# Fixed slots for the modulation weights, and zero-padded rotary keys, in a one-layer decoder kernel

## The chip, the core and the metric

The kernel runs on one core of a Trainium2 chip. The core has a matrix engine (TensorE, PE in the tables; its weight loads are listed apart as PEld), a vector engine (DVE), an activation engine (ACT), a general engine (GpSimd, POOL) and a queue engine that here only issues transfers (SP). All of them work from on-chip memory with 128 partitions (rows); the matrix engine writes to eight accumulator banks of 128 x 512 float32, which DVE and ACT read. The metric is the device time of one execution in microseconds (us); smaller is better. It is given as the median of several executions. The profile shows one execution.

## What is computed

One decoder layer on 512 tokens with 2048 channels, batch 1, all in float32:

```
mod = silu(c) @ W_ada + b_ada             # 6 vectors of 2048: shift, scale, gate, twice
h   = RMSNorm(x) * (1 + scale_a) + shift_a
proj = h @ W_in                           # q/k/v of mixer A, its indexer, latents of mixer B, two gates
o_A = sparse attention: 8 heads, 2 kv heads, the 128 best keys per query by an indexer
o_B = latent attention: 8 heads, query and key = 128 plain + 64 rotated dimensions
y   = (sigmoid(g_a) * (o_A @ W_pA) + sigmoid(g_b) * (o_B @ W_pB)) @ W_o
x   = x + gate_a * y
h   = RMSNorm(x) * (1 + scale_f) + shift_f
x   = x + gate_f * (W_down( silu(conv(h W_up)_gate) * conv(h W_up)_value ))
```

The change touches two places of this: the logits of mixer B, which for each head are the sum of a product over 128 plain dimensions and one over 64 rotated dimensions,

```
logits[q, s] = sum_{d<128} qn[q, d] kn[s, d] + sum_{r<64} qr[q, r] kr[s, r]
```

and the way in which parts of `W_ada` (2048 x 12288) reach the vector engine.

## The kernel before

Large products are made of three matrix-engine passes, since each float32 operand is split into a rounded part (`hi`) and a rest (`lo`), and hi*hi, hi*lo and lo*hi are summed (`mm3`, lines 141 to 144). A weight tile of 128 x 1024 is loaded by SP into one of five raw buffers, split by ACT (line 130) and DVE (line 131) into one of three hi/lo buffers, and then used (`wtile`, lines 117 to 135). Attention itself (logits, transposes, product with the values) uses plain float32 matmuls, each of which the trace shows as two records.

The rest of the on-chip memory is 81 slots of 128 x 512 float32. `get()` (lines 69 to 76) takes, among the free slots, the one that has rested longest by a counter that stands still during the stages told here, so that free slots are in fact taken first in, first out; `put()` (lines 81 to 86) gives one back. The program text only fixes which slot each tile has and what depends on what. The order of the instructions on each engine is made when the program is built, by a planner that simulates the engines: it takes whatever is ready, by priority, and priority is the order in the text, except that weight tiles are moved 4000 places ahead. After that each engine and each queue runs its list strictly in order and waits where an operand isn't there.

The stages, in order of time in the profile: the projections (to about 430 us), mixer A with the gate projections (to about 780), mixer B's attention together with the product `W_pA` (about 785 to 1060), the product `W_pB` (to about 1130), the product `W_o` (to about 1307), then the feed-forward part (to the end). These parts are touched or spoken of:

- **Modulation stream.** Two thirds of `W_ada` aren't needed at once. `ada_stream` (lines 726 to 755) is a generator that goes through 16 blocks of 512 columns; each of its steps loads two tiles of 128 x 512 (256 KB each; one pair) and has DVE multiply each by its element of silu(c) and add it to an accumulator (lines 745 and 747, three accumulators in turn). `ticker(rate)` calls it `rate` times per weight step of the product running. A pair goes either into two slots (line 735, when `ada_in_slots` is set) or into one of the five raw weight buffers (line 739). The slots are those that `get()` gives next, so the stream walks through the whole free list. Slots are used in mixer A and, from line 1245 on, for the products `W_pB` and `W_o`; the raw buffers in between.
- **Flush.** When a block's accumulator is finished, `flush_cols` (lines 777 to 794) splits it, sums it over the partitions with two matmuls (lines 782 and 783) into the bank that is passed in (the fourth of the next half of the banks) and takes the result out with DVE (lines 790, 793 and 298). The product that follows uses the same bank.
- **Rotated parts of mixer B.** `up_pair(hp)` (lines 1135 to 1208) makes queries and keys of two heads. The rotated parts of both heads stand side by side, 64 columns each, in one tile, and are transposed together, so that `kTr` and `qTr` hold the first head in rows 0 to 63 and the second in rows 64 to 127 (`kTr` at lines 1161 and 1167 to 1170). In `attend_pair` (lines 1210 to 1225), each logit block is a matmul over 64 rows of these tiles (line 1217) and one over the 128 rows of the plain part (line 1218), into the same bank.
- **Attention of a head** (`attend_p`, `attend_pv`, lines 677 to 714): four logit blocks, with 512, 384, 256 and 128 keys; scaled, masked and searched for the extreme by DVE (line 689), exponentiated by ACT (690), normalised by DVE (691, 692), transposed (700), copied out (703, 705), multiplied with the values (708), copied out and split (710, 711).
- **Loads by POOL.** POOL issues stores and reloads of intermediate tiles (lines 713, 714, 804, 805, 822, 1263 to 1265, 1304) and computes small powers (`rsqrt_mean`, line 246), all in one queue.

Of the kernel before, what the change touches and what calls it, by code (L numbers as in the profile page):

```python
# [14 lines left out]
AF = mybir.ActivationFunctionType  # L15
# [16 lines left out]
def trunk_layer_kernel(  # L32
# [48 lines left out]
    def put(*ts, lag=2):  # L81

        for t in ts:
            i = held.pop(id(t))
            rested[i] = clock[0] + lag
            free.append(i)
# [440 lines left out]
    b = bank[7]  # L527
# [194 lines left out]
    ada_acc = [get(), get(), get()]  # L722

    ada_in_slots = [False]

    def ada_stream():
        for n, cb in enumerate(ada_blocks):
            assert len(pend) < 3
            acc = ada_acc[n % 3]
            for kp in range(8):  # L730
                if ada_in_slots[0]:
                    ts = [get(), get()]
                    for i in range(2):
                        k = kp * 2 + i
                        SP.dma_start(ts[i], w_ada[k * P:(k + 1) * P, cb * 512:(cb + 1) * 512])
                else:
                    raw = rawq.popleft()
                    t = raw[:, 0:1024].rearrange("p (k n) -> p k n", k=2)
                    SP.dma_start(t, w_ada[kp * 2 * P:(kp + 1) * 2 * P, cb * 512:(cb + 1) * 512]
                                 .rearrange("(k p) n -> p k n", p=P))  # L740
                    ts = [t[:, 0], t[:, 1]]
                for i in range(2):
                    k = kp * 2 + i
                    if k == 0:
                        V.tensor_scalar(acc, ts[i], c_act[:, 0:1], None, op0=ALU.mult)
                    else:
                        V.scalar_tensor_tensor(acc, ts[i], c_act[:, k:k + 1], acc,  # L747
                                               op0=ALU.mult, op1=ALU.add)
                if ada_in_slots[0]:
                    put(*ts)  # L750
                else:
                    rawq.append(raw)
                yield None
            pend.append((cb, acc))
            done[0] += 1
# [379 lines left out]
    def up_pair(hp):  # L1135
# [22 lines left out]

        lin_tm(w_mkv_up, hp * 512, 512, kvT, 2, MM, ev_up)
        kT = [get(), get()]  # L1160
        kTr = get()
        for a in range(2):
            b = at_bank()
            for tb in range(4):
# [2 lines left out]
        b = at_bank()  # L1167
        for tb in range(4):
            PE.transpose(b[:, tb * P:(tb + 1) * P], kr[:, tb * P:(tb + 1) * P], ident)
        A.activation(kTr, b, AF.Copy)  # L1170
        put(*kn)
        put(kr)

# [36 lines left out]
    def attend_pair(hp):  # L1210
        qT, qTr, kT, kTr, vv, nsc_b, two = pairs.pop(hp)
        for a in range(2):
            rs = slice(a * 64, (a + 1) * 64)

            def qk(o, qb, S, a=a, rs=rs, qT=qT, qTr=qTr, kT=kT, kTr=kTr):
                qs = slice(qb * P, (qb + 1) * P)
                PE.matmul(o[:, :S], qTr[rs, qs], kTr[rs, :S], start=True, stop=False)
                PE.matmul(o[:, :S], qT[a][:, qs], kT[a][:, :S], start=False, stop=True)  # L1218

            attend(qk, lambda qb: Z[:, 384 - qb * P:512], lambda qb, a=a, n=nsc_b: n[:, qb, a:a + 1],  # L1220
                   lambda kc, a=a, vv=vv, two=two: two(vv, kc)[:, a, :], *(ob_d[hp * 2 + a] if hp < 3 else (None, None)))
        put(*vv)
        put(*kT)
        put(*qT)
        put(kTr, qTr)


    pa_d = [dram.tile([P, T], F32, name=f"pa{k}") for k in range(KD)]
# [13 lines left out]
        if hp < 2:  # L1242
            up_pair(hp + 2)
    attend_free("pt")
    ada_in_slots[0] = True
    for t in oa:
        put(*t)
    for t in kvT + mqT:
# [80 lines left out]
        lin_tm(w_o, db * 512, 512, mg, KD, bk, ev_o(db), tick=ticker(TO))  # L1329
    while next(stream, 0) is None:  # L1330
        pass
    for db in range(3):
        x1_T(db, half() if db % 2 == 0 else bk)
        if db == 0:
            for t in mg:
                put(*t)
# [289 lines left out]
```

## Time and profile before

| | |
|---|---|
| median of 3 executions | 2678.14 us (2677.77 to 2680.52) |
| the profiled execution | 2681.41 us |
| its span, first to last instruction | 2679.6 us |
| PE busy | 2604.5 us (97%), 17168 matmul records |
| DVE busy | 2175.6 us (81%) |
| ACT busy | 1265.8 us (47%) |
| POOL busy | 364.2 us (14%) |
| moved by the DMA engines | 464.31 MB, mean 173 GB/s |
| mean granted clock of the matrix engine | 0.99 |

Busy shares are sums over the span. A matmul record begins when the matmul is issued and its end is modelled, so records overlap, and time in which the matrix engine waits inside a record counts as busy. Where an engine waits, the rows name what ended the wait ("<-"); "issue" is a wait for nothing that the profile shows. In rows of groups, the numbers after the bar are the busy time in us, the mean of one instruction in ns and the idle time before them in us.

### The profile page before, as it was taken

The page shows a single profiled execution, that of the slowest core. Times are in us where ns is not written, and L with a number is a line of the kernel's source. Part 1 is how long each engine was busy: PE and PEld are TensorE (multiplying, and loading weights), DVE is VectorE, ACT ScalarE, POOL GpSimd, SP SyncE. Part 2 cuts the span into 40 slices and gives each one's busy share as a digit, 9 for nine tenths or more (in the row PEclk, how much of TensorE's full clock was granted, in tenths as well). Part 3 has the DMA queues.
Part 4 walks back from the last instruction along what each step waited for, and adds up shares of the span by engine and source line. Part 5 has one row for each costly group of instructions (what it writes and reads, how often), then busy time and mean ns, then how long its engine had stood idle before and what let it go on. Part 6 is the DMA issues. An engine that isn't in the chain of part 4 may idle for free.

```text
span 2679.6 us, 44954 instructions
## 1 busy us (share of the span) xinstructions
PE 2604.5 (97%) x17168; PEld 2344.1 (87%) x17168; DVE 2175.6 (81%) x3491; ACT 1265.8 (47%) x1967; POOL 364.2 (14%) x663
## 2 busy tenths in 40 slices
PE   6999999999999999999999999999999999999999
PEld 5777687778997766788789999999999998999999
DVE  7976976779878676984569989989989889878787
ACT  4333434334435556322445555555555556655454
POOL 1000011010022223100100000000001024413120
PEclk8999899999999999999999999999999999999999
DMA  9953136674675587982424343344344447867563
GB/s 341 342 160 104 32 107 204 201 223 155 198 248 171 168 264 246 315 289 93 142 79 136 119 143 124 119 146 126 121 139 148 132 147 212 214 159 205 142 204 116
DMA packets 215661, 464.31 MB, mean 173 GB/s; under 512 B 23786, under 2 KB 65156, under 8 KB 215444
## 3 DMA queue, kind: packets, MB, share of 16 engines
q1 hardware_dynamic: 170260, 344.93, 40.3%
q0 software_dynamic: 45152, 116.50, 15.0%
q8 instruction: 134, 2.20, 0.3%
q14 instruction: 83, 0.68, 0.1%
q10 hardware_dynamic: 32, 0.01, 0.0%
HBM read 397.11 MB, written 64.23 MB: 172 GB/s over the span
## 4 chain that ended last, share of the span: by engine, by line
PE 71%; issue 12%; DMA 8%; DVE 6%; POOL 2%; ACT 2%; SPq 0%; POOLq 0%; DVEq 0%; ACTq 0%
PE bank L1072 13%; PE bank L1074 13%; PE bank L1073 13%; PE bank L142 9%; PE bank L143 9%; PE bank L144 9%; DMA slot<-in_w_ada 3%; DMA x<-slot 2%; DVE whl L139 1%; DMA raw<-in_w_ada 1%; DVE slot L747 1%; DVE slot L572 0%; PE bank L708 0%; DVE raw L968 0%; PE bank L1218 0%
## 5 line engine op out<-in xcount | busy, mean ns | idle before, releaser
L1072 PE MATMUL bank<-slot,whl 128*128 128x256 f32 x3920 | 1104.7, 283 | 24.2 <-ACT slot L972 6.4
L1073 PE MATMUL bank<-slot,whl 128*128 128x256 f32 x3920 | 1101.0, 282 | 0.2 <-DVE slot L139 0.2
L1074 PE MATMUL bank<-slot,whl 128*128 128x256 f32 x3920 | 1090.4, 282 | 7.0 <-DVE whl L139 7.0
L138 ACT ACTIVATE whl<-raw 128x1024 fp32r<-128x1024 f32 (+2 forms) x560 | 532.6, 953 | 620.3 <-PE bank L1073 402.2
L1072 PEld LDWEIGHTS bank<-slot,whl 128*128 128x128 f32 x3920 | 740.4, 189 | 31.4 <-ACT slot L972 9.0
L1073 PEld LDWEIGHTS bank<-slot,whl 128*128 128x128 f32 x3920 | 741.8, 189 | 0.6 <-DVE slot L139 0.5
L1074 PEld LDWEIGHTS bank<-slot,whl 128*128 128x128 f32 x3920 | 734.1, 189 | 8.3 <-DVE whl L139 8.2
L139 DVE TENSOR_TENSOR whl<-raw,whl 128x1024 fp32r<-128x1024 f32 (+2 forms) x560 | 606.0, 1088 | 123.5 <-ACT whl L138 120.8
L130 ACT ACTIVATE whl<-raw 128x1024 fp32r<-128x1024 f32 (+4 forms) x182 | 187.4, 1031 | 381.6 <-PE bank L144 190.5
L968 DVE TENSOR_TENSOR raw<-raw 128x1024 f32<-128x1024 f32 (+2 forms) x320 | 347.5, 1086 | 7.8 <-DMA raw<-in_w_ups 4.9
L131 DVE TENSOR_TENSOR whl<-raw,whl 128x1024 fp32r<-128x1024 f32 (+4 forms) x182 | 216.0, 1188 | 155.2 <-ACT whl L130 149.7
L143 PE MATMUL bank<-whl,slot 128*128 128x512 f32 (+2 forms) x768 | 297.3, 388 | 0.9 <-DVE whl L131 0.9
L142 PE MATMUL bank<-whl,slot 128*128 128x512 f32 (+2 forms) x768 | 292.2, 392 | 4.2 <-ACT slot L409 3.6
L144 PE MATMUL bank<-whl,slot 128*128 128x512 f32 (+2 forms) x768 | 293.0, 386 | 0.0
L142 PE MATMUL bank<-slot,whl 128*128 128x512 f32 (+1 forms) x656 | 264.3, 407 | 7.1 <-DVE slot L790 4.8
L143 PE MATMUL bank<-slot,whl 128*128 128x512 f32 (+1 forms) x656 | 264.0, 403 | 1.8 <-DVE slot L711 1.8
L144 PE MATMUL bank<-slot,whl 128*128 128x512 f32 (+1 forms) x656 | 259.1, 402 | 0.0
L747 DVE SCALAR_TENSOR_TENSOR slot<-slot,c_act,slot 128x512 f32<-128x512 f32 x203 | 148.6, 747 | 37.2 <-DMA slot<-in_w_ada 35.6
L142 PEld LDWEIGHTS bank<-whl,slot 128*128 128x128 f32 x768 | 146.3, 191 | 35.4 <-ACT slot L409 3.7
L143 PEld LDWEIGHTS bank<-whl,slot 128*128 128x128 f32 x768 | 146.4, 191 | 29.8 <-DVE whl L131 1.4
L144 PEld LDWEIGHTS bank<-whl,slot 128*128 128x128 f32 x768 | 144.8, 189 | 29.3 <-issue 0.4
L142 PEld LDWEIGHTS bank<-slot,whl 128*128 128x128 f32 (+1 forms) x656 | 123.5, 188 | 38.1 <-DVE slot L790 5.7
(288 smaller groups left out, 2730.3 us busy)
## 6 DMA issues: line engine op xcount, KB each, us to landing
slot<-in_w_ada SPq DMA_DIRECT2D x344, 256.0 KB, 5.6
raw<-in_w_ups SPq DMA_DIRECT2D x160, 512.0 KB, 5.1
raw<-in_w_in SPq DMA_DIRECT2D x50, 512.0 KB, 3.7
raw<-in_w_down SPq DMA_DIRECT2D x64, 384.0 KB, 3.8
raw<-in_w_down SPq DMA_DIRECT2D x64, 320.0 KB, 3.8
slot<-f POOLq DMA_DIRECT2D x154, 128.0 KB, 4.0
f<-slot POOLq DMA_DIRECT2D x66, 256.0 KB, 5.1
raw<-in_w_gs SPq DMA_DIRECT2D x32, 512.0 KB, 4.6
```

What stands on the lines that cost most here:

```text
L130: A.activation(hi, raw[:, :w], AF.Copy)
L131: V.tensor_tensor(lo, raw[:, :w], r32(hi), ALU.subtract)
L138: A.activation(dst_hi, src, AF.Copy)
L139: V.tensor_tensor(dst_lo, src, r32(dst_hi), ALU.subtract)
L142: PE.matmul(o, lh, rh, start=first, stop=False)
L143: PE.matmul(o, lh, rl, start=False, stop=False)
L144: PE.matmul(o, ll, rh, start=False, stop=last)
L747: V.scalar_tensor_tensor(acc, ts[i], c_act[:, k:k + 1], acc, op0=ALU.mult, op1=ALU.add)
L968: V.tensor_tensor(o[:, :W], a[:, :W], b[:, :W], op)
L1072: PE.matmul(o, wh[:, ks], rh, start=first and k == 0, stop=False, skip_group_check=True)
L1073: PE.matmul(o, wh[:, ks], rl, start=False, stop=False, skip_group_check=True)
L1074: PE.matmul(o, wl[:, ks], rh, start=False, stop=last, skip_group_check=True)
```

## The change

Two edits. First, when the second run of slots begins (line 1245), the modulation stream takes six slots and keeps them: a pair takes the two that stand first in a queue of six and puts them back at its end, so that a pair always follows the pair three before it in the same two slots. The six go back to the free list when the stream has ended, after the product `W_o`. Second, `kTr` becomes two tiles, one per head, each 128 rows high: GpSimd fills the rows of the other head with zeros, ACT copies the head's own 64 rows in, and the matmul over the rotated part runs over all 128 rows, with the queries of both heads in `qTr` as before.

```diff
     ada_in_slots = [False]
+    ada_ring_on, ada_ring = [False], deque()
...
                 if ada_in_slots[0]:
-                    ts = [get(), get()]
+                    ts = [ada_ring.popleft(), ada_ring.popleft()] if ada_ring else [get(), get()]
                     for i in range(2):
                         k = kp * 2 + i
                         SP.dma_start(ts[i], w_ada[k * P:(k + 1) * P, cb * 512:(cb + 1) * 512])
...
-                if ada_in_slots[0]:
+                if ada_ring_on[0]:
+                    ada_ring.extend(ts)
+                elif ada_in_slots[0]:
                     put(*ts)
...
         kT = [get(), get()]
-        kTr = get()
+
+        kTr = [get(), get()]
+        for a in range(2):
+            G.memset(kTr[a][(1 - a) * 64:(2 - a) * 64], 0.0)
...
-        A.activation(kTr, b, AF.Copy)
+        for a in range(2):
+            A.activation(kTr[a][a * 64:(a + 1) * 64], b[a * 64:(a + 1) * 64], AF.Copy)
...
         for a in range(2):
-            rs = slice(a * 64, (a + 1) * 64)
-
-            def qk(o, qb, S, a=a, rs=rs, qT=qT, qTr=qTr, kT=kT, kTr=kTr):
+
+            def qk(o, qb, S, a=a, qT=qT, qTr=qTr, kT=kT, kTr=kTr):
                 qs = slice(qb * P, (qb + 1) * P)
-                PE.matmul(o[:, :S], qTr[rs, qs], kTr[rs, :S], start=True, stop=False)
+                PE.matmul(o[:, :S], qTr[:, qs], kTr[a][:, :S], start=True, stop=False)
                 PE.matmul(o[:, :S], qT[a][:, qs], kT[a][:, :S], start=False, stop=True)
...
-        put(kTr, qTr)
+        put(*kTr, qTr)
...
     attend_free("pt")
-    ada_in_slots[0] = True
+
+    ada_in_slots[0] = ada_ring_on[0] = True
+    ada_ring.extend(get() for _ in range(6))
     for t in oa:
         put(*t)
...
     while next(stream, 0) is None:
         pass
+    put(*ada_ring)
     for db in range(3):
```

## The prediction

> **What bounds the kernel now.** I read the page first, then the span cut at the stages that the change touches, then who waited for whom on each engine there, and last the chain of waits.
>
> ```profile
> span 2679.6 us, 44954 instructions
> PE 2604.5 (97%) x17168; PEld 2344.1 (87%) x17168; DVE 2175.6 (81%) x3491; ACT 1265.8 (47%) x1967; POOL 364.2 (14%) x663
> PE 71%; issue 12%; DMA 8%; DVE 6%; POOL 2%; ACT 2%; SPq 0%; POOLq 0%; DVEq 0%; ACTq 0%
> ```
>
> The matrix engine is busy for 97% and makes 71% of the chain that ended last. The stretches, each with span, then busy us of PE, PEld, DVE, ACT and POOL, granted clock, DMA share and GB/s:
>
> ```profile
> 820.00:1015.00 195.00, 195.00 (x869) 142.50 (x868) 138.78 (x398) 101.13 (x201) 52.24 (x81) 1.00 0.66 208
> 1015.00:1060.00 45.00, 39.79 (x167) 28.94 (x167) 27.09 (x51) 26.73 (x38) 13.81 (x25) 1.00 0.77 255
> 1100.00:1120.00 20.00, 15.59 (x62) 12.19 (x61) 17.93 (x29) 4.45 (x7) 3.21 (x6) 0.91 0.77 244
> 1120.00:1300.00 180.00, 180.00 (x776) 145.37 (x775) 110.36 (x147) 48.35 (x66) 8.66 (x14) 1.00 0.58 194
> ```
>
> In mixer B's attention (820 to 1015) PE has no visible idle time, and DVE, ACT and POOL have 56, 94 and 143 of 195 us left. A us taken from PE there is a us taken from the stage, as long as the chains through the other engines keep up. The tail of attention (1015 to 1060) has 5.2 us of PE idle, 1100 to 1120 another 4.4, and W_o from 1120 on none. So the two edits fall on different things: the padded keys on a stretch that PE bounds, the six slots on two holes in PE's work.
>
> What PE does in its full stretch (line 1217 is the matmul over rotated rows, 1218 over plain rows, 708 and 898 are float32 matmuls among 128-row matmuls only; after the bar busy us and mean ns; 898 is from 400 to 785 us):
>
> ```profile
> L1217 PE MATMUL bank<-slot,slot 64*128 64x512 f32 x16 | 8.9, 635 | 0.0
> L1218 PE MATMUL bank<-slot,slot 128*128 128x512 f32 x16 | 8.9, 638 | 0.0
> L898 PE MATMUL bank<-slot,slot 128*128 128x512 f32 x16 | 8.2, 592 | 0.0
> PEld bank L1218 <- issue: 12.3, 24, 0.8
> PEld bank L1217 <- issue: 8.5, 23, 0.8
> 842.85 1.05 PE bank L1217 x2
> 843.90 1.06 PE bank L1218 x2
> 865.73 2.16 PE bank L708 x8
> 900.11 0.84 PE bank L1218 x2
> 912.57 1.70 PE bank L1217 x4
> ```
>
> The last five are pieces of the chain (start, us). Both matmuls of a logit block are longer than the same shape of mixer A, and their weight loads, alone among PE's, wait for "issue" at nearly every block. The chain prices it. The eight records of line 708 are two each with 512, 384, 256 and 128 columns, 1280 columns in 2.16 us, so 0.86 us for two records of 512 and 0.65 for 384. Line 1217 at 512 takes 1.05, 1218 takes 1.06 and, at 384, 0.84: 0.19 us more each time. Four records of 1217 in a row, 512 and 384, take 1.70 = 0.86 + 0.65 + 0.19, so it is paid once per run of one height, not per matmul: PE pays it when the matmul goes from 128 rows to 64 and again when it goes back. The 128-row matmul pays after a 64-row one and nowhere else (708 doesn't), so it is not a cost of float32.
>
> The Trainium skill, TensorEngine Tiling (Array Packing), section Tiling Modes, states that a change of tiling mode drains the engine; the trace agrees, with 0.19 us beside it. The skill's TensorE: Matmul & The Clock Gate puts the drain at about 175 ns; by that figure an estimate for the padding would be 62 x 0.175 = 10.9 us instead of the 11.8 below.
>
> **The padded keys, step by step.** Eight heads with four logit blocks are 32 matmuls of line 1217 (64 records). In one place two stand together, as above, so 31 changes to 64 rows and 31 back. Padded, both matmuls have 128 rows and neither change happens; rows don't set a matmul's time (635 against 638 ns above), so the padding itself costs PE nothing. Gain: 62 x 0.19 = 11.8 us. Where it may not arrive: two of the 32 blocks lie in the tail, in which PE waits anyway (2 x 0.38 = 0.8 us), and a chain logits, DVE, ACT, DVE, transposes that PE's detour now hides could show. From both sides: all of it (11.8), or, if every freed us became a wait, 0. I take 11, near the upper end, since only some 12 us in 195 go and DVE has 56 to spare there.
>
> What it adds:
>
> ```profile
> L239 POOL MEMSET slot<- x1: 544/544/544, 6.3 to 6.3; 128x512 bf16 x1
> L246 POOL TENSOR_TENSOR rs<-rsm,mhalf 128x2 f32<-128x2 f32 x36 | 31.3, 877 | 64.4 <-DVE rsm L245 61.8 <-DVE ropetmp L512 2.4
> L1170 ACT ACTIVATE slot<-bank x4: 596/604/626, 817.5 to 938.4; 128x512 f32<-128x512 f32 x4
> L1217 PE MATMUL bank<-slot,slot x64: 272/481/694, 834.0 to 1033.3; 64*128 64x384 f32 x16, 64*128 64x512 f32 x16, 64*128 64x256 f32 x16, 64*128 64x128 f32 x16
> ```
>
> Eight fills of 64 x 512 float32 on POOL. The one fill in the trace took 0.54 us for as many columns of half the width, so 0.5 to 1.1 us each, 9 us at most on an engine that idles 143. Queued behind a fill are the powers of line 246, for which DVE, and then the transposes on PE, wait. That can only be felt at the first two pairs, before attention covers it: four fills, 0 to 4.4 us. I take 0.5, since a fill needs no operand and the planner can put it in a gap. A fill also waits for the last reader of its slot, which is the longest-rested one: nothing. ACT makes two copies where it made one, four more of 0.6 us: 2.4 us of ACT time, hidden, because ACT is half idle and the first copy (817.5) is 16 us ahead of its first reader (834.0); without that cover it would cost 0.6 per pair. Each live pair holds a slot more: with a first-in-first-out list this shortens the rest of every other slot a little; no price.
>
> **The six slots, step by step.** What the stream's slots wait for now (first the transfers' queue from 1040 to 1200, then DVE from 940 to 1210, then PE from 1000 to 1130):
>
> ```profile
> SPq L735 <- DVE slot L747: 18.9, 20, 2.6
> SPq L735 <- DVE slot L1268: 15.4, 6, 10.4
> SPq L735 <- PE bank L783: 10.3, 3, 4.1
> DVE slot L747 <- DMA slot<-in_w_ada: 9.0, 5, 4.5
> PE bank L142 <- DVE slot L790: 4.8, 2, 4.4
> PE bank L143 <- DVE slot L711: 1.8, 1, 1.8
> 1055.06 3.12 DVE L747 SCALAR_TENSOR_TENSOR slot<-slot,c_act,slot 128x512 f32<-128x512 f32 x4 [4.50 <-DMA slot<-in_w_ada]
> 1058.10 0.68 DVE L711 TENSOR_TENSOR slot<-bank,slot 128x512 fp32r<-128x512 f32 x1
> 1113.90 0.75 DVE L747 SCALAR_TENSOR_TENSOR slot<-slot,c_act,slot 128x512 f32<-128x512 f32 x1 [2.00 <-DMA slot<-in_w_ada]
> 1114.58 0.68 DVE L790 TENSOR_TENSOR slot<-bank,ident 128x512 f32<-128x512 f32 x1
> ```
>
> A pair's transfer waits for whoever had its slot before, gates (1268) among them; the multiply-add on DVE waits for the transfer; and behind it in DVE's list stand 711 and 790, for which PE waits. That is the whole of the two holes that a late pair makes: 1.8 us at 1058 and 4.4 us at 1111. The second costs more than it lasts: 62 records in 20 us where W_o has 776 in 180, so 24 too few at 0.23 us, 5.6 us, because the clock afterwards is lower (0.91). With six slots a pair waits only for the second multiply-add three pairs before. Best case: both holes go, 7.4 us. Worst case: the stream has three pairs ahead instead of the whole list, and a late transfer stops DVE more often.
>
> ```profile
> slot<-in_w_ada SPq DMA_DIRECT2D x82, 256.0 KB, 6.3
> L783 PE MATMUL bank<-slot,ones_r x16: 387/394/796, 487.0 to 1311.3; 128*128 128x512 f32 x16
> L747 DVE SCALAR_TENSOR_TENSOR slot<-slot,c_act,slot 128x512 f32<-128x512 f32 x89 | 64.2, 748 | 9.6 <-DMA slot<-in_w_ada 9.0
> ```
>
> Three pairs in turn need one landing (6.3 us) and two multiply-adds (1.5 us) per round, some 8 us, or 2.6 us a pair. Wanted are 1.25 pairs per weight step of 24 matmuls at 0.23 us, one pair in 4.4 us. So six slots can feed the stream, with 13 us of lead against 8 needed. The starving end is bounded by the same price, 5.6 us for each stop that has a flush behind it. Between 7.4 gained and 5.6 lost I take 1.5 gained: the hole at 1058 goes, the other moves. Nothing is added on SP's list: the same transfers; weight loads behind a waiting pair have five raw buffers of cover. The six slots out of the list leave gate and x reloads (POOL) less choice; they have the four weight steps of a block, 4 x 24 x 0.23 = 22 us, ahead of their use, hidden.
>
> **The sum.** 2681.4 (the profiled execution: 2679.6 of span and 1.8 around it) - 11 + 0.5 - 1.5 = 2669.4. That execution lies 3.3 us above the median of the runs shown, so against the median 2678.1 - 12 = 2666 us.
>
> **The rivals.** (a) Both holes close as well: 2678 - 11 + 0.5 - 7.4 = 2660. For it: both have a slot's release at their root; against it: the second pair (1113.9) was late by only 2 us, in a stretch where transfers fill 0.77 of the DMA engines. (b) The freed time comes back as waits in the tail, which ACT, DVE and the transfers set and not PE (40 of 45 us busy, 0.77 DMA): of 12 us some 3 to 4 remain, 2675. For it: the tail's chain is one head's latency. Against it: that chain starts when its logits are done, and these come 10 us earlier too. (c) Slower: with three pairs ahead, DVE stands in the stream's transfer in front of a flush. Of the sixteen flushes (line 783, the last at 1311) eight come after 1020; from three stops on, at 5.6 each, the padding is used up (-11 + 17 = +6): 2684. For it: landings are 6.3 us under load, and the planner's list puts a multiply-add where its simulation has the landing. Against it: the lead above. (d) The change of height isn't the cause and the 0.19 stays: 2678. Against it: line 708 and line 898, float32 too, without it.
>
> (e) Two half-height matmuls of different heads could overlap, and padding ends that. Half of the rotated matmuls' own time would be lost, eight heads x 2.16 / 2 = 8.6 us: 2666 + 8.6 = 2675. The records speak against it: no 64-row record is shorter or overlaps more than its 128-row partner. That the two halves of the rows can work side by side, up to twice as fast, is what the Trainium skill's TensorEngine Tiling (Array Packing), sections Overview and When to Use Tiling, states.
>
> **Chances.** The forecast as summed 0.50 (2661 to 2672), (a) 0.20, (b) 0.11, (c) 0.13, (d) 0.04, (e) 0.02. Range: from 2656, below (a) by its rounding and the 0.8 of the tail, to 2681, which takes in (b), (d), (e) and the mild end of (c); 0.05 below, 0.1 above. A difference under 0.2% (5.4 us) can't be told from none here. Faster by more: forecast, (a) and a little of (b), 0.74. Within: the rest of (b), (d), (e) and the mild end of (c), 0.14. Slower: 0.12.
>
> **What would show it.** Right: matmuls of line 1217's successor at 592 ns for 512 columns, no "issue" wait before either load, two records of 512 in 0.86 us of chain; the stretch from the first logits to the last product shorter by about 11 us; transfers of the stream waiting for line 747 only. Wrong: the same extra 0.19 us, new idle time on PE before transposes (700), or DVE waiting longer than 9 us for the stream's transfers with 790 or 131 behind it. The forecast fails if the planner makes another order of the lists in which a weight split or a flush comes late; the trace of before can't show that.

## The result and the profile after

| | before | after |
|---|---|---|
| median of 4 executions each | 2677.95 us (2675.53 to 2680.52) | 2663.82 us (2661.51 to 2667.96) |
| ratio after to before, 95% interval | | 0.9949 [0.9932, 0.9966] |
| the profiled execution | 2681.41 us | 2663.55 us |

The kernel became faster by 14.1 us. The forecast was 2666 us. The first lines of the profile of the changed kernel, with span, busy time and instructions of each engine:

```profile
span 2661.8 us, 44939 instructions
PE 2595.5 (98%) x17168; PEld 2351.5 (88%) x17168; DVE 2174.4 (82%) x3491; ACT 1262.4 (47%) x1967; POOL 365.6 (14%) x671
```

PE lost 9.0 us of busy time (2604.5 to 2595.5) and the span lost 17.8, so over the whole span about half of it is time inside PE's records and half is idle time between them; these are sums over gains and losses, which the account below parts. The same four stretches as before (stretch and span, then busy us of PE, PEld, DVE, ACT and POOL, granted clock, DMA share and GB/s):

```profile
820.00:1015.00 195.00, 188.16 (x867) 144.53 (x866) 149.09 (x411) 106.09 (x207) 54.03 (x89) 1.00 0.68 222
1015.00:1060.00 45.00, 44.76 (x200) 35.48 (x200) 38.03 (x68) 25.22 (x42) 12.30 (x23) 1.00 0.96 342
1100.00:1120.00 20.00, 20.00 (x87) 16.14 (x86) 16.81 (x24) 7.08 (x9) 3.98 (x8) 1.00 0.98 331
1120.00:1300.00 180.00, 179.35 (x799) 145.06 (x798) 98.15 (x130) 51.71 (x80) 7.61 (x13) 1.00 0.50 165
```

Both places where PE stood idle are full now: 44.76 of 45 us (39.79 before), and 20.00 of 20 us with 87 records (15.59 with 62), at a granted clock of 1.00 instead of 0.91. But in attention, where PE had no visible idle time, it now stands for 6.8 of 195 us. The groups of the matmuls from 820 to 1060 us, the waits of their weight loads from 780 to 1040, and pieces of the chain (start, us) tell what the padding did:

```profile
L1223 PE MATMUL bank<-slot,slot 128*128 128x512 f32 x16 | 8.4, 606 | 0.1
L1224 PE MATMUL bank<-slot,slot 128*128 128x512 f32 x16 | 8.2, 592 | 0.0
...
PEld bank L708 <- issue: 3.6, 15, 0.2
PEld bank L1224 <- issue: 3.3, 14, 0.2
...
PEld bank L1223 <- issue: 0.2, 1, 0.2
...
841.38 0.86 PE bank L1223 x2
842.24 0.87 PE bank L1224 x2
```

The rotated matmul (1223, was 1217) has gone from 635 to 606 ns and the plain one (1224, was 1218) from 638 to 592; the pair of 512 columns takes 0.86 and 0.87 us instead of 1.05 and 1.06. The waits for "issue" at the plain load have fallen from 12.3 us in 24 to 3.3 in 14, and the longest from 0.8 to 0.2 us; at the rotated load they have fallen from 8.5 us in 23 to 0.2 in one. What is left at 1224 is what the loads of the product with the values (708) have too, 3.6 us in 15 here and 3.4 in 14 before the change. So the prediction's "alone among PE's" was not right; only the long waits stood at the logits alone. What PE now waits for, from 820 to 1330 us, is short:

```profile
PE bank L700 <- DVE mn L689: 4.0, 3, 2.0
...
PE bank L700 <- DVE slot L692: 2.1, 2, 1.1
...
PE bank L142 <- DVE slot L793: 0.2, 1, 0.2
```

The flush (line 790 before, 793 now) made PE wait for 4.8 us, and makes it wait for 0.2; the wait of 143 for 711 is gone. In their place stand the transposes of attention (700), which wait for DVE's search and normalisation (689, 692) for 6.1 us instead of 2.3.

**One account for all runs.** The table below cuts the stretch from the first logits of mixer B to the last product `W_o` into three parts. It is worked out from the trace's matmul records: between the ends of two records that follow each other lies the usual spacing of that shape (0.231 us for a hi/lo pass of 512 columns, 0.429 for a float32 record of 512); what is over it counts, up to 0.2 us, as a change of row height if the two records differ in rows, and otherwise as a wait. The boundary between the two kinds of wait is the last product with the values (708). The ratios are to runs of the kernel before beside them.

| kernel | median us | ratio [95%] | stretch | changes of height | waits in attention | waits behind it |
|---|---|---|---|---|---|---|
| before | 2677.95 to 2680.86 | 1 | 474.0 | 12.1 | 5.6 | 10.0 |
| after | 2663.82 | 0.9949 [0.9932, 0.9966] | 460.2 | 0 | 12.1 | 1.7 |
| after, again | 2662.23 | 0.9929 [0.9914, 0.9944] | 458.1 | 0 | 10.0 | 1.7 |
| padding alone | 2674.42 | 0.9981 [0.9969, 0.9994] | 475.9 | 0 | 19.3 | 10.2 |
| slots alone | 2673.63 | 0.9978 [0.9968, 0.9988] | 470.8 | 12.1 | 10.6 | 1.7 |
| held stream | 2668.45 | 0.9956 [0.9943, 0.9968] | 466.6 | 0 | 8.8 | 11.3 |
| spare slot | 2678.31 | 0.9992 [0.9983, 1.0000] | 472.4 | 12.0 | 8.1 | 6.0 |
| two slots | 2698.64 | 1.0062 [1.0039, 1.0084] | 501.2 | 0 | 14.4 | 40.3 |
| four slots | 2664.69 | 0.9942 [0.9930, 0.9955] | 461.0 | 0 | 8.9 | 5.7 |
| twelve slots | 2676.39 | 0.9979 [0.9968, 0.9991] | 469.1 | 0 | 14.4 | 8.3 |
| late sigmoids | 2659.77 | 0.9921 [0.9903, 0.9938] | 454.5 | 0 | 6.4 | 1.7 |

What is left of each stretch is PE's work, 446.3 to 446.5 us in all of them. From before to after: changes of height -12.1, waits in attention +6.4, waits behind it -8.3, together -14.0; the stretch shows -13.8. The other 4 us of the span's 17.8 lie outside the stretch: the first logits start 1.4 us earlier (832.6 instead of 834.0), and what follows `W_o` is some 2.5 us shorter, by about as much as it differs between the two profiles of the changed kernel (2.2 us). The stretches are those of one profiled execution each and the medians those of several; single executions of one kernel differ by several us, so the columns show where time lies, and the ratios how much it is. Between the two profiles of the changed kernel the waits in attention differ by 2.1 us (12.1 and 10.0), and the profiled execution of padding alone lies 3.5 us above its median, that of twelve slots 5.4 below.

### The profile page after: what moved, and what is told of

It is laid out like the page before. It is cut to its first block, busy times and chain, and to the rows that moved or that the text cites. A ratio compares the mean times of both kernels' runs of the same rounds, so it can differ in the third digit from the quotient of the medians.

```text
span 2661.8 us, 44939 instructions
## 1 busy us (share of the span) xinstructions
PE 2595.5 (98%) x17168; PEld 2351.5 (88%) x17168; DVE 2174.4 (82%) x3491; ACT 1262.4 (47%) x1967; POOL 365.6 (14%) x671
## 4 chain that ended last, share of the span: by engine, by line
PE 60%; issue 6%; DMA 5%; DVE 4%; ACT 2%; POOL 1%; SPq 0%; POOLq 0%; DVEq 0%; ACTq 0%
PE bank L1075 14%; PE bank L1077 14%; PE bank L1076 14%; PE bank L142 5%; PE bank L143 5%; PE bank L144 5%; DMA slot<-in_w_ada 2%; DVE whl L139 1%; DMA raw<-in_w_ada 1%; DMA x<-slot 1%; DVE raw L971 1%; DVE slot L748 1%; DMA gate<-slot 0%; ACT whl L138 0%; PE bank L708 0%
## 5 line engine op out<-in xcount | busy, mean ns | idle before, releaser
L142 PEld LDWEIGHTS bank<-whl,slot 128*128 128x128 f32 x768 | 146.0, 191 | 33.9 <-ACT slot L409 3.3
```

Of the source, the lines that this page charges most:

```text
L142: PE.matmul(o, lh, rh, start=first, stop=False)
```

## The experiments

**Each part alone.** The changed kernel without the six slots, and then the changed kernel without the padding.

```diff
-    ada_in_slots[0] = ada_ring_on[0] = True
-    ada_ring.extend(get() for _ in range(6))
+    ada_in_slots[0] = True
...
-    put(*ada_ring)
```

> Only the padded keys; the modulation stream takes its slots from the free list as before. Theory A (the two edits act on different stretches, and the change from 128 to 64 rows and back is what the padding saves): 62 changes at 0.19 us go, the holes of 1.8 and 5.6 us behind late pairs stay (they may move), so 10 to 12 us faster, ratio 0.9955 to 0.9963; both matmuls of a logit block at 592 ns for 512 columns. Theory B (the whole gain of 14 us comes from the padding, through the planner's new order): 13 to 15 us faster, and no matmul waits for lines 790 or 711 of before. Theory C (the freed matrix-engine time comes back as waits unless the six slots are there too): under 5 us faster.

Measured: 2674.42 us (2668.09 to 2681.40), ratio 0.9981, some 5 us less than before (0.19% of 2679). The changes of height are gone to the last one, 12.1 us, and still only 5 arrive: the theory by which the padding brings 10 to 12 us by itself is wrong, and the one that gave it under 5 us, because the freed time comes back as waits, is near. In the account its waits in attention rise by 13.7 us (5.6 to 19.3), in an execution slower than its median, and the holes behind attention stay (10.0 and 10.2). PE's waits from 780 to 1130 us, and then who kept POOL from issuing reloads, from 930 to 1130:

```profile
PE bank L142 <- DVE slot L793: 5.2, 1, 5.2
PE bank L1223 <- DVE slot L703: 3.4, 2, 2.8
PE bank L142 <- ACT slot L824: 3.2, 3, 1.9
...
PE bank L142 <- ACT slot L710: 2.3, 1, 2.3
```

```profile
POOL pa L825 <- ACT slot L824: 16.1, 2, 11.1
...
POOL slot L1272 <- DVE slot L748: 7.7, 2, 7.5
```

```profile
ACT slot L824 <- DMA pa<-slot: 8.4, 2, 4.5
```

A load of a gate (line 1272 of this kernel) waits up to 7.5 us because its slot was a slot of the stream, whose multiply-add (748) is late. Stores (825) stand on the same queue, and ACT's copies (824), which need the slots that those stores free (the last row, ACT's waits in the same window), come late for PE. That the one delay hands itself on to the other is argued from these rows. It isn't what is new here: in the kernel before, such rows stood already in POOL's waits from 930 to 1130 us, and waits for the stream's multiply-adds add up to 19.7 us there and to 20.1 with the padding alone. New are PE's waits for copies by DVE and ACT (703, 824, 710). The row of before:

```profile
POOL slot L1265 <- DVE slot L747: 12.6, 4, 10.1
```

```diff
-        kTr = [get(), get()]
-        for a in range(2):
-            G.memset(kTr[a][(1 - a) * 64:(2 - a) * 64], 0.0)
+        kTr = get()
...
-                PE.matmul(o[:, :S], qTr[:, qs], kTr[a][:, :S], start=True, stop=False)
+                PE.matmul(o[:, :S], qTr[rs, qs], kTr[rs, :S], start=True, stop=False)
```

> Only the six slots; rotated keys of two heads share a tile as before. Theory A (two holes of 1.8 and 5.6 us close, but the stream then runs ahead into the attention tail, where its multiply-adds and their waits for transfers stand in front of the normalisation, about 5 us of new waits before the transposes): net 2 to 3 us faster, ratio 0.9985 to 0.9995, 62 row changes still there at 0.19 us. Theory B (the six slots alone give the best case, both holes gone and nothing new): 7 us faster, ratio 0.997. Theory C (with the attention still slowed by the row changes, three pairs ahead starve DVE): slower.

Measured: 2673.63 us (2671.35 to 2675.09), ratio 0.9978, 5.9 us less than before, between the two theories and nearer to the one by which both holes close. The waits behind attention fall from 10.0 to 1.7 us; the waits in attention rise from 5.6 to 10.6. In PE's waits from 820 to 1330 us none for a flush's result is left; the longest is:

```profile
PE bank L1222 <- ACT slot L705: 2.8, 1, 2.8
```

The two parts alone bring 5.1 and 5.9 us in ratios' terms (0.0019 and 0.0022 of 2679), 11 together; both at once bring 14 (0.0051) in the first comparison and 19 (0.0071) in the second. That they help one another is likely: the padding brings 5 us where the stream shares the free list and, as the difference of ratios, 8 us (0.0029) in the first comparison and 13 (0.0049) in the second where it doesn't. But the first comparison's interval for the whole change, 9 to 18 us, takes in the sum of 11; only the second's, 15 to 23, lies above it.

**The whole change again,** for a comparison on the chip on which the other numbers of slots were run.

> The changed kernel once more, beside the variants below on the same chip. All theories: ratio to before 0.993 to 0.997. From the first logits to W_o's last evacuation its profile should again have about 446 us of matrix-engine work, no row changes and 12 to 16 us of waits; if the waits move by more than 4 us from the first profile, differences of that size between single profiles tell nothing.

Measured: 2662.23 us (2661.31 to 2663.75), ratio 0.9929. The intervals of the two comparisons overlap at 0.9932 to 0.9944.

**Is it the change of height?** In the kernel before, the plain part of the logits is cut to the same 64 rows as the rotated part. This leaves out half of the plain dimensions in mixer B's logits; the columns, and with them the matmuls' own time, stay.

```diff
-                PE.matmul(o[:, :S], qT[a][:, qs], kT[a][:, :S], start=False, stop=True)
+                PE.matmul(o[:, :S], qT[a][rs, qs], kT[a][rs, :S], start=False, stop=True)
```

> The kernel before, but with the plain part of mixer B's logits over the same 64 rows as the rotated part, so half of the plain dimensions is left out of these logits. Both matmuls of a block then have 64 rows; the same number of matmuls, the same columns. Theory A (PE pays 0.19 us where the row height changes, whichever matmul stands there): line 1218 no longer pays and goes to the mean of line 898, 592 ns at 512 columns; line 1217 still pays on entry; and the matmul or transpose behind line 1218 pays on leaving, so the number of changes and the time stay as before, 2674 to 2682 us. Theory B (the cost belongs to the second matmul of an accumulated pair or to a 64-row matmul as such): line 1218 pays still, or both pay at each instruction.

Measured: one time, 2671.72 us, 2 us below the range foretold. The groups from 820 to 1060 us, and then pieces of the chain (start, us):

```profile
L1217 PE MATMUL bank<-slot,slot 64*128 64x512 f32 x16 | 8.8, 628 | 0.0
L1218 PE MATMUL bank<-slot,slot 64*128 64x512 f32 x16 | 8.2, 596 | 0.0
```

```profile
838.16 1.05 PE bank L1217 x2
839.22 0.86 PE bank L1218 x2
840.07 0.43 PE bank L143
...
843.97 0.62 PE bank L1217 x2
...
855.90 0.43 PE bank L1217 x2
...
856.77 0.43 PE bank L144
```

The plain part has fallen to 596 ns without gaining a row: it no longer follows a matmul of another height. The entry is still paid by 1217 (1.05 instead of 0.86), and the way back now by whatever follows: one record of 143 or 144 with 0.43 instead of 0.23. Where one logit block follows another (855.90), 1217 pays nothing either: 0.43 us for two records of 256 columns, where 0.62 are taken at 843.97, after a 128-row matmul. So neither float32 nor a half-height matmul costs more in itself; the change between heights does. Blocks adjoin more often in this kernel's list, which is why the account finds 8.8 us of changes (46 at 0.19) instead of 12.1. The Trainium skill, TensorEngine Tiling (Array Packing), section Tiling Modes, says that it is the change of mode, not just of the tile, that drains the engine. These rows agree for the mode; the blocks that adjoin here are those of one head, in the same half of the rows, so they don't test the tile.

**Does it matter that the stream runs ahead?** In the changed kernel, the stream's multiply-adds in the six slots are held back until the last head's output is split (line 711).

```diff
-        V.tensor_tensor(ol, ob, r32(oh), ALU.subtract)
+        last_pv[0] = V.tensor_tensor(ol, ob, r32(oh), ALU.subtract)
...
+                    with tc.issue_after(last_pv[0].ins) if ada_ring_on[0] else nullcontext():
```

> Both edits, and in addition every multiply-add of the stream in its six slots is put behind the last head's split (the DVE instruction of line 711) on DVE's list; the transfers of the first three pairs may still go early. Theory A (the new waits before the transposes in the attention tail come from multiply-adds that run ahead there): those waits, some 5 us at 1000 to 1016 us in the changed kernel, shrink to 1 to 2 us, and if DVE has room for the stream behind the attention, the kernel is 2 to 4 us faster than the changed one, ratio to before about 0.9935. Theory B (these waits are the head's own latency, laid bare by the shorter matrix-engine work): they stay, and the time is that of the changed kernel, 0.995. Theory C (DVE is full during the product W_pB): a later flush makes a hole there, and the kernel is slower than the changed one by up to 6 us.

Measured: 2668.45 us (2664.94 to 2672.78), ratio 0.9956. By the end of attention 151 of the 256 multiply-adds are done, against 182 with the change and 174 before. The waits in attention fall from 12.1 (10.0 in the second profile) to 8.8 us, so the run-ahead probably costs something there; but the waits behind attention come back, 11.3 us instead of 1.7:

```profile
PE bank L142 <- ACT whl L130: 4.1, 1, 4.1
...
PE bank L142 <- DVE slot L795: 2.4, 2, 1.6
```

So the theory by which holding back brings 2 to 4 us more is wrong. With six slots but the stream held back, further than it was before the change, the holes behind attention are open again: the slots don't close them without the run-ahead, which moves DVE's work for the stream to where PE has other things to do. That it is worth more than it costs is likely from the medians (2668.5 against 2663.8 and 2662.2), though the interval overlaps both of the whole change's.

**How many slots.** Two, four and twelve instead of six; for twelve and two:

```diff
-    ada_ring.extend(get() for _ in range(6))
+    ada_ring.extend(get() for _ in range(12))
```

> The changed kernel with twelve slots for the stream instead of six (six pairs ahead instead of three). Theory A (what helps is that the stream's slots are apart from those of the gate loads and of the attention, not their number): same as the changed kernel within 0.15%. Theory B (the lead of three pairs is what limits; more lead closes waits for the stream's transfers): 2 to 5 us faster than the changed kernel, DVE's waits for these transfers under 4 us from 940 to 1125 (8.5 in the changed kernel). Theory C (fewer slots for the rest make gate and x loads late): slower by 3 us or more.

> The changed kernel with two slots, one pair, for the stream: each pair's transfers wait for the pair before. By the forecast's rates a round of one landing (5 to 6 us) and two multiply-adds (1.5 us) is some 7 us, against one pair wanted in 4.4 us. Theory A (a stream with fewer pairs ahead than the rate needs starves, and flushes come late): the last multiply-add falls behind W_o (later than 1290), DVE waits for the stream's transfers over 60 us in all, and the kernel is 20 to 60 us slower than before, 2700 to 2740. Theory B (the planner knows the rate and puts the multiply-adds where nothing waits behind them): within 10 us of before.

> The changed kernel with four slots, two pairs, for the stream. By the forecast's rates a round of two pairs is 7 us, one pair in 3.5 us, against one wanted in 4.4 us: just enough. Theory A (the lead has to cover landing and multiply-adds, and every slot beyond that only takes from the gate loads): within 0.2% of six slots, ratio to before 0.993 to 0.996, no starving. Theory B (the lead shrinks the time gradually, as two slots showed): halfway between two and six, about 0.999 to 1.001, with waits of 10 to 20 us behind the attention.

Measured: two 2698.64 us (ratio 1.0062, 17 us slower than before), four 2664.69 (0.9942), six 2663.82 and 2662.23, twelve 2676.39 (0.9979). With two slots DVE stands in the stream's transfers (its waits from 940 to 1330 us), and the weight splits behind them come late for PE (its waits from 820 to 1330):

```profile
DVE slot L748 <- DMA slot<-in_w_ada: 92.5, 49, 5.3
```

```profile
PE bank L143 <- DVE whl L131: 14.7, 8, 5.1
...
PE bank L142 <- DVE slot L793: 4.6, 2, 2.7
```

That is the starving that the prediction named as its slow rival, and its place: a split (131) and not only a flush (793) behind the waiting multiply-add. The price, 17 us against the kernel before, is below the 20 to 60 us that was expected; against four slots it is 32 us by the ratios (0.0120). Four slots are as good as six by their intervals, though DVE waits longer for the stream (from 940 to 1210 us, four slots, then six):

```profile
DVE slot L748 <- DMA slot<-in_w_ada: 34.3, 24, 3.2
```

```profile
DVE slot L748 <- DMA slot<-in_w_ada: 10.0, 11, 2.2
DVE slot L746 <- DMA slot<-in_w_ada: 4.3, 1, 4.3
```

24 short waits of 1.4 us cost nothing that can be measured; 49 of 1.9 us, over the longer window, go with 32 us. With twelve slots DVE waits for the stream least of all (2.9 us at line 748 in that window), and the time is worse than with six by 0.0050, 13 us. The tiles that are reloaded then get what is left of the free list; that this is the cause is likely from two rows of one profile, whose execution was among the faster ones. POOL from 940 to 1125 us and PE from 820 to 1330:

```profile
POOL slot L1272 <- PE bank L786: 18.7, 1, 18.7
```

```profile
PE bank L142 <- DMA slot<-obh: 3.7, 1, 3.7
```

A gate's reload stands 18.7 us for a slot that a flush still reads, and what is queued behind it on POOL with it. The first matmul of a product then waits 3.7 us for a reloaded tile of attention's output.

**Is it the demand for slots that eats the padding's gain?** In the kernel before, each pair of heads takes one more slot, which nobody uses, as the padded keys do.

```diff
-        kTr = get()
+        kTr, spare = get(), get()
...
-        put(kTr, qTr)
+        put(kTr, spare, qTr)
```

> The kernel before, and each pair of heads holds one more slot that nothing uses, as long as it holds its rotated keys: the padded keys' demand for slots without the padding. Theory A (padding alone keeps only 5 of its 12 us because the extra slots shift who follows whom on the free list, so gate loads and stores on GpSimd's queue come later): 3 to 8 us slower than before, with more waits of PE in the attention (5.6 us before) and the 12 us of row changes unchanged. Theory B (the extra slots cost nothing; padding alone loses its gain because the chains through DVE, ACT and the transfers are what sets the end of the attention there): within 2 us of before, waits as before.

Measured: 2678.31 us (2675.03 to 2680.98), ratio 0.9992 [0.9983, 1.0000]. In the list of the kernel before, a slot less does nothing to the time. So a shortage of slots by itself is not the price that takes the 7 us that the padding alone doesn't bring (12.1 - 5); the account finds them as waits in attention. Whether the slot costs something once the changes of height are gone, and what the fills and the second copy do to the order of the lists, no run tested. That PE then needs everything earlier while DVE, POOL and the shared slots keep their pace is the likely reading; it is argued and not isolated by a run.

**What the transposes now wait for.** In the changed kernel the chain from DVE's search through ACT's exponential back to the transposes is what PE waits for. ACT changes its function table there again and again; its groups from 930 to 1045 us:

```profile
L690 ACT ACT_TABLE_LOAD x6 | 7.7, 1283 | 0.1
...
L1275 ACT ACT_TABLE_LOAD x4 | 5.1, 1283 | 0.1
L1274 ACT ACT_TABLE_LOAD x3 | 3.8, 1283 | 0.1
```

These are 13 loads, 16.7 us, between exponentials (690) and the gates' sigmoids (1274, 1275); nine of them, not seven, lie from 989 to 1026 us. The kernel before had more of them in the same window, 19 loads or 24.4 us, with less waiting of PE:

```profile
L690 ACT ACT_TABLE_LOAD x9 | 11.5, 1283 | 0.5 <-DVE mn L689 0.3
...
L1267 ACT ACT_TABLE_LOAD x5 | 6.4, 1283 | 0.1
L1266 ACT ACT_TABLE_LOAD x5 | 6.4, 1283 | 0.1
```

So the loads didn't come with the change; at most they cost more where PE arrives earlier. The experiment lets the sigmoids start only after the last exponential.

```diff
-            A.activation(p, p, AF.Exp, bias=mn, scale=-1.0, accum_out=su)
+            last_exp[0] = A.activation(p, p, AF.Exp, bias=mn, scale=-1.0, accum_out=su)
...
-            A.activation(g, g, AF.Sigmoid)
-            A.activation(b, b, AF.Sigmoid)
+            with tc.issue_after(last_exp[0].ins):
+                A.activation(g, g, AF.Sigmoid)
+                A.activation(b, b, AF.Sigmoid)
```

> The changed kernel, with every sigmoid of a gate placed behind the last exponential of the attention on ACT's list. In the changed kernel ACT changes its table seven times between exponential and sigmoid from 989 to 1026 us, at 1.28 us each. Theory A (the waits of PE before the transposes in the tail, some 8 us, come partly from ACT's table changes between the exponentials of a head): two changes are left, the waits in the attention fall by 3 to 6 us, and the kernel is 2 to 5 us faster than the changed one. Theory B (they come from DVE's list, where the stream's multiply-adds stand before the extremes and the normalisation): same as the changed kernel. Theory C (the sigmoids are then late for the first evacuations of W_pB): up to 5 us slower.

Measured: 2659.77 us (2657.45 to 2664.53), ratio 0.9921 [0.9903, 0.9938], the lowest median of all. The groups from 930 to 1045 us have one table load, and PE's waits from 820 to 1330 us none for the search (now line 690); the longest in sum are 3.3 us for the normalisation (693):

```profile
L1276 ACT ACT_TABLE_LOAD x1 | 1.3, 1283 | 0.0
```

The waits in attention fall from 10.0 and 12.1 to 6.4 us, about what they were before the change. Against the changed kernel beside it the median is 2.5 us lower, but the executions overlap (2657 to 2665, and 2661 to 2664): that the loads, laid bare by the earlier logits, are part of what came back is possible, and not shown by the times.

**The same remedy elsewhere.** The indexer's logits in mixer A also run over 64 rows. Their keys were padded to two tiles of 128 rows in the same way, on top of the late sigmoids.

```diff
-            mm3(b[:, :S], qh[ps, qs], ql[ps, qs], kiT[0][ps, :S], kiT[1][ps, :S], True, True)
+            mm3(b[:, :S], qh[:, qs], ql[:, qs], kh[:, :S], kl[:, :S], True, True)
```

> The kernel with late sigmoids, and the indexer's keys padded to 128 rows in the same way as the rotated keys (two zero-padded copies, made with a column of zeros and ones as scale, two more operations on ACT and DVE and two more slots there). In the changed kernel some 20 changes between 64 and 128 rows remain in the indexer between 200 and 310 us, 0.2 to 0.3 us each, 5 us together. Theory A (each change is PE time and PE bounds that stretch): 3 to 5 us faster than late sigmoids alone, ratio to before 0.990 to 0.991, no 64-row matmul left. Theory B (the indexer is bound by the chain matmul, ACT, DVE of one accumulator and not by PE): no change within 0.1%.

Measured: 2661.80 us (2654.73 to 2664.63), ratio 0.9926 [0.9910, 0.9942]: no gain beside the late sigmoids alone. The matmuls of 64 rows are gone, but the first logits of mixer B start at 837.0 us, against 832.7 with late sigmoids alone. The trace names a price that neither theory had: in the indexer neighbouring heads lie in different halves of the rows, and their 64-row matmuls run side by side. With late sigmoids alone, then with the padded keys (start, us):

```profile
255.43 0.28 PE L143 MATMUL bank<-slot,slot 64*128 64x256 f32 x2
255.55 0.28 PE L144 MATMUL bank<-slot,slot 64*128 64x256 f32 x2
```

```profile
253.23 0.28 PE L143 MATMUL bank<-slot,slot 128*128 128x256 f32 x1
253.34 0.28 PE L144 MATMUL bank<-slot,slot 128*128 128x256 f32 x1
```

The two records of the first row start within 0.01 us of each other and the next two 0.12 us later; with padded keys every 0.12 us starts one. Worked out from the spacing of the records as in the table above, an estimate: with late sigmoids alone 45 such pairs save PE 6.3 us, and the 22 changes of height cost it 4.5, so padding takes away more PE time here than it gives. DVE is busy for 34.8 of the 35 us from 280 to 315 us with late sigmoids alone, so the chain that the second theory named may set the end of the stage all the same; no run parts the two.

## Why the prediction was right, and where it wasn't

The sum was -11 for the padding, +0.5 for the fills and -1.5 for the slots, 12 in all; measured are 14 and 19. The result is inside the range and on the forecast's side. Its terms did not all come out, and that the total is so near is partly luck, as the end of this section says.

- **The change of height (0.19 us, 62 times): right.** The account has 62 changes, 61 of them with 0.19 to 0.20 us, 12.05 us together, and none after. Cutting the plain part to 64 rows moved the price to the neighbour, as a price of the change between heights must. Rival (d) falls with it, and rival (e) too for mixer B: no matmul became longer when the halves went (635 to 606 ns). But the reading against (e), that no 64-row record overlaps more than its 128-row partner, holds for these lines alone: in the indexer of the same kernel 64-row records of two heads do run side by side, and there the padding brought nothing.
- **"I take 11, near the upper end, since only some 12 us in 195 go and DVE has 56 to spare": right only together with the slots.** With the slots in place the padding brings 8 to 13 us by the two comparisons; alone it brings 5. The step that failed is the reason given. DVE's spare time did not decide; waits in the chains did, for copies by DVE and ACT with the padding alone and for DVE's search and normalisation with both parts. Rival (b), freed time that comes back as waits, is what happened to the padding alone (+13.7 us of waits in attention in its profile, the execution being 3.5 us above the median).
- **"Between 7.4 gained and 5.6 lost I take 1.5 gained: the hole at 1058 goes, the other moves": too small.** Alone the slots bring 5.9 us. Both holes closed: waits behind attention fell by 8.3 us, rival (a)'s 7.4 and a little more. They go with 5 us more of waits in attention, where the stream now runs ahead (186 multiply-adds at its end in that run, 182 with both parts, 174 before). The forecast missed both and had their difference half right: 8.3 - 5.0 = 3.3 in the account, 5.9 in the times, with an interval from 3 to 9.
- **What the slots do to the reloads.** "The six slots out of the list leave gate and x reloads less choice" was put down as a cost, hidden. POOL's reloads waited up to 10.1 us for the stream's multiply-adds before, and not at all after: no row of POOL waiting for 748 is left between 930 and 1130 us. But POOL's waits there add up to 146.0 us before, 139.5 after and 146.8 with the slots alone: the reloads now wait for the gates' own arithmetic (1276, 1285) instead. That this was a gain in time isn't shown. What the run with the held stream shows is that the holes don't close unless the stream runs ahead in attention, which the forecast's sum didn't have.
- **"Six slots can feed the stream, with 13 us of lead against 8 needed": right.** The landing takes 5.2 us instead of 6.3 (from 1040 to 1200 us):

```profile
slot<-in_w_ada SPq DMA_DIRECT2D x68, 256.0 KB, 5.2
SPq L736 <- DVE slot L748: 40.2, 59, 3.3
```

  The stream's transfers wait for 748 above all, where "only" was foretold, and no longer for gates (1268 before) or flush matmuls; 8.2 us for a landing, 5.0 for 746, the first multiply of a block, and 4.0 for the last step of a flush (298) are left. Rival (c) has its threshold: four slots feed the stream, two don't, and then the kernel is 17 us slower than before by the mechanism that was named.
- **A sign that says little without its condition.** DVE waiting longer than 9 us for the stream's transfers, "with 790 or 131 behind it", was to speak against the forecast. It waits 14.3 us (10.0 for 748 and 4.3 for 746), and with four slots 34.3 for 748 alone, at no cost that can be measured; PE waits for a flush for 0.2 us. With two slots the splits (131) stand behind the waits and PE waits for them. A wait counts by what stands behind it and when that is due.
- **The fills and copies: right.** Eight fills took 0.52 us each, within the 0.5 to 1.1 (the row below), and the eight copies 0.59 each; the first copy is at 816.6 us, 16.0 ahead of its first reader at 832.6. The 0.5 us that the sum charges for the fills is not seen in any run by itself.

```profile
L1167 POOL MEMSET slot<- x8: 518/521/547, 773.1 to 894.2; 64x512 f32 x8
```

- **What would show it.** The stretch from the first logits to the last product with the values is 216.6 us before and 202.7 after, 13.9 shorter where 11 was said, but that is no proof: some 8 us of it is other matmuls, such as those of `W_pA`, that PE now does behind the stretch (927 matmul records in it before, 891 after). The rest is 12.1 us of changes less 6.4 of new waits. The rotated matmul came to 606 ns where 592 was said. New idle time before the transposes (700) was named as a sign against it, and came: 6.1 us of waits instead of 2.3. It ate part of the gain and not all.

So the total was near because two errors of opposite sign met: the slots closed 8.3 us of waits where 1.5 was taken, and 6.4 us came back as waits in attention where 0.8 was taken. What is still open: why the planner's list for the padding alone has so many more waits in attention than the list before. The runs show the waits and the slots' last users, not how the choice was made.

## What to carry to other kernels

A 64-row matmul alone among 128-row matmuls pays on the way in and on the way out, here 0.19 us each; zeros in the other half cost 0.52 us a tile on an engine that is mostly idle and take it away. Where 64-row matmuls of both halves stand next to each other, look first whether they run side by side: then zeros take that away too, as in the indexer. A stream that walks through a shared first-in-first-out list couples its lateness to everyone who gets its slots next; a few slots of its own cut that and let it run ahead, and their number has a lower and an upper bound (here two starve it, four or six suffice, and twelve are slower again, probably because they starve the others). Two edits that work on one stretch can't safely be priced apart: count what each does to the chains that the other shortens.

## What was not expected of the hardware

- The executions of one kernel differ by more than expected: the kernel before spread over 16 us in one comparison (17 executions, 2671.3 to 2687.7), padding alone over 13 (11, 2668.1 to 2681.4), twelve slots over 10.6 (12, 2668.9 to 2679.5), the change with six slots over 6.5 (4) and 2.4 (6, 2661.3 to 2663.8). The spare-slot kernel, which shares the list as the kernel before does, spread over 6.0 (12), so the sharing alone doesn't explain it. What does wasn't tested.
- A change of ACT's table costs what its row says, 1283 ns, and no more in this trace: the load starts at 988.98 us, when the split before it has just ended (988.97), and after it, at 990.26, the sigmoid starts at 990.28. All 14 loads of the changed kernel from 780 to 1320 us start within 0.02 us of the end before them, and in 11 the next operation starts 0.01 us behind the load; in the other three it waits for DVE's search.

```profile
987.92 1.05 ACT L130 ACTIVATE whl<-raw 128x1024 fp32r<-128x1024 f32 x1
988.98 1.28 ACT L1275 ACT_TABLE_LOAD   x1
990.28 0.63 ACT L1275 ACTIVATE slot<-slot 128x512 f32<-128x512 f32 x1
```

  The Trainium skill, ScalarE: Activation LUTs, section What ACT_TABLE_LOAD costs, has the same 1283 ns and a drain of about 1380 ns on top, 2.66 us for each switch. For 13 switches that would be an estimate of 34.6 us instead of 16.7; the trace shows the smaller.
